# A decoder kernel on one Trainium2 core: eleven feed-forward slices and two down steps of layer 0 as seven block products

## The chip, the core and the metric

The kernel runs on one core of a Trainium2 chip. The core has a matrix engine (TensorE, PE in the profile; PEld is its weight load), VectorE (DVE), ScalarE (ACT), GpSimd (POOL) and SyncE (SP). PE reads operands from the on-chip memory SBUF and writes results to PSUM, which has eight banks of 128 x 512 float32. Sixteen DMA engines move data between DRAM and SBUF or within DRAM; SP issues nearly all loads and stores, POOL issues the indirect page loads and the sums described below. Each engine works through its own list of instructions in order and waits on semaphores for the others. The metric is device time in microseconds (us), the median of several executions.

## What is computed

A two-layer decoder step on 1024 prompt tokens and 8 sample tokens of width 1024. Layer 0 has a gated recurrence (HGRN2) and attention to 256 memory tokens, layer 1 has stick-breaking attention and memory attention; each layer ends with a SwiGLU feed-forward block of 22 slices of 128 (D_FF = 2816). Cut to the part that changes:

```python
def swiglu(h, w_gu, w_down):
    gate, up = jnp.split(h @ w_gu, 2, axis=-1)
    return (jax.nn.silu(gate) * up) @ w_down

# in run_trunk, for each layer l
h = h + rmsnorm(mix, g[1])
h = h + rmsnorm(swiglu(rmsnorm(h, g[2]), w_gu[l], w_down[l]), g[3])
```

All of it is float32. The kernel reaches that accuracy by splitting each operand into a rounded part (fp32r) and a remainder and by adding three products (high x high, high x low, low x high).

## The kernel before

The 1024 tokens are worked on in two halves, `g = 0` (512 tokens) and `g = 1` (512 tokens and the 8 samples, 520 columns in two pieces of 260). Layer 0 of the second half is woven with layer 1 of the first half, and so on: `weave` takes generators with numbers and advances the one that is furthest behind, so the program text of several stages is mixed. A scheduler then orders each engine's instructions; the text's order is its priority.

A feed-forward block runs over five parts, `PARTS = [(0, 5), (5, 5), (10, 4), (14, 4), (18, 4)]`, given as first slice and number of slices. For each slice the plain class `ffn` calls `proj` for gate and up (`L220` holds all its matmuls): it loads weights with `split_w`, four 128 x 128 tiles (256 KB) at a time into one of five `wraw` buffers, casts them on ACT (`L206`) and subtracts on DVE (`L207`), and multiplies them with the eight x tiles. `silu` is made of Exp and Ln, so that ScalarE keeps one table of functions. After the slices of a part, its down step multiplies them with `w_down` and adds into R.

The last block of the program (layer 1, second half) uses the class `ffn_w` instead. There gate and up of a slice are seen as a 2 x 2 block matrix (two halves of the 1024 inputs; gate and up) times a 2 x 2 block matrix of x (two halves of the inputs, two halves of the columns). Seven products in place of eight give the four results: each product multiplies a block or a sum of blocks of the weights by a block or a sum of blocks of x. `gate_up_w` does that with 260 columns and four 128 x 128 tiles per product (`L527`); `down_w` (`L706`) does the same for a down step with pairs of slices. The sums of x blocks (`sums_w`) are made on DVE once, those of slices (`put_sum`) as they come. Silu comes from ScalarE's own table there, which is loaded before (`L492`) and changed back behind (`L757`).

The weight sums are made in DRAM ahead of time. `weight_sums` (gate and up) and `down_sums` yield eight steps for each part, in `summed`: a copy of one block into a DRAM tile, or an accumulating DMA on top of it. Each step is paced by a one-column token: ACT copies a column of a recent result into an `rr` tile of three buffers (`L612`), POOL copies that into `mk` (`L613`), and POOL then issues the DMA (`L616` accumulates, `L618` copies). A step waits for the DMA whose result it reads. Before, only layer 1 has sums: down sums of parts 1 to 3 run beside `a1.core` (24 steps), gate and up sums beside `b0.sb`, `b0.mem` (16) and beside parts 2 to 4 of the layer 0 block of the second half (24, from about 1206 to 1410 us).

In `ffn_w` the raw weights go into the five `wraw` buffers and, from part 1 on, every other one into a half of a free `apool` tile; the split weights go into five `wspl` and some of four `cpool` tiles.

Of the kernel before, what the change touches and what calls it, by code (L numbers as in the profile page):

```python
# [18 lines left out]
P = 128  # L19
# [5 lines left out]
def tile_decoder(  # L25
# [169 lines left out]

    def split_w(W, k0, nk, m0):
        out = []
        for a in range(0, nk, 4):
            n = min(4, nk - a)
            raw = wraw.tile([P, 4, P], F32, tag="w", name=nm("w"))  # L200
            nc.sync.dma_start(
                raw[:, :n, :],
                W[(k0 + a) * P : (k0 + a + n) * P, m0 : m0 + P].rearrange("(k p) m -> p k m", p=P),
            )
            ws = wspl.tile([P, 2, 4, P], F32R, tag="ws", name=nm("ws"))
            nc.scalar.copy(ws[:, 0, :n, :], raw[:, :n, :])  # L206
            nc.vector.tensor_sub(ws[:, 1, :n, :], raw[:, :n, :], ws[:, 0, :n, :].bitcast(F32))  # L207
            for i in range(n):
                out.append((ws[:, 0, i, :], ws[:, 1, i, :]))
        return out  # L210
# [84 lines left out]
    def sums_w(xs, ops):  # L295
# [29 lines left out]
    def YT():  # L325
        return xpool.tile([P, 2, NG[1]], F32R, tag="x0", name=nm("y"))
# [172 lines left out]
    def gate_up_w(l, f, ops, spl, raws, pair=None):  # L499

        h, n = PW[1], NG[1]
        part, o = part_of(f)
        gate, up = f * P, DFF + f * P
        src = [
            (w_gu[l][0:512, gate : gate + P], 0), (sums[l][part][0][:, o : o + P], 4), (sums[l][part][1][:, o : o + P], 5),
            (w_gu[l][512:D, gate : gate + P], 1), (sums[l][part][2][:, o : o + P], 6), (sums[l][part][3][:, o : o + P], 2),
            (w_gu[l][512:D, up : up + P], 3),
        ]

        def weight(j):  # L510
            r = raws()
            nc.sync.dma_start(r, src[j][0].rearrange("(k p) m -> p k m", p=P))
            return r.rearrange("p k m -> p (k m)")

        def split(src):
            w = spl()
            nc.scalar.copy(w[:, 0, :], src)  # L517
            nc.vector.tensor_sub(w[:, 1, :], src, w[:, 0, :].bitcast(F32))  # L518
            return w

        def product(ps, j, first=False):
            w = split(weight(j))
            i = src[j][1]
            for k in range(4):
                x = ops[k][i]
                for wi, (wj, xi) in enumerate(((0, 0), (0, 1), (1, 0))):
                    nc.tensor.matmul(  # L527
                        ps[:, :h], w[:, wj, k * P : (k + 1) * P], x[:, xi, :],
                        start=(first and k == 0 and wi == 0), stop=(k == 3 and wi == 2), skip_group_check=True,
                    )  # L530
# [41 lines left out]
        return mt  # L572

# [25 lines left out]
    def down_sums(l, parts, after):  # L599
        for i in parts:  # L600
            t = [tc.dram_tile([P, 2, 512], F32, name=nm("dsum")) for _ in range(4)]
            dsums[i] = t
# [18 lines left out]
    dsums = {}  # L621
    htok, done = [], []

    PARTS = [(0, 5), (5, 5), (10, 4), (14, 4), (18, 4)]

    class ffn_w:


        def __init__(self, l, x, plain):
# [3 lines left out]
            self.sums = sums_w(x, self.ops)  # L633
# [23 lines left out]
        def gate_up(self, pi, j0=0, j1=None):  # L657
# [3 lines left out]
            for j in range(j0, nf if j1 is None else j1):  # L661
# [7 lines left out]
                else:  # L669
                    pair = pairs[j // 2] if self.block(pi) and j < 4 else None  # L670
                    mids.append(gate_up_w(l, f0 + j, self.ops, self.spl, self.raws, pair))
                yield

        def down_w(self, pi, f0, pairs, extra):
            l, n, h, R = self.l, NG[1], PW[1], self.R
            a11, a12, a21, a22 = down_blocks(l, f0)
            s1, s2, s3, s4 = dsums[pi]
            src = ((a11, 0), (s1, 4), (s2, 5), (a12, 1), (s3, 6), (s4, 2), (a22, 3))
            for m0 in (0, 2):
                ms = (m0, m0 + 1)  # L680
                acc = [[Q(i) for i in range(4)] for _ in ms]

                def weight(rows):
                    r = self.raws().rearrange("p k m -> p (k m)")
                    nc.sync.dma_start(r.rearrange("p (t c) -> p t c", t=2), rows[:, :, m0 * P : (m0 + 2) * P])
                    w = self.spl()
                    split_to((w[:, 0, :], w[:, 1, :]), r)
                    return w

                def slice_of(q, hf, a, first=False):  # L690
                    for i in range(2):
                        o = hf * 256 + i * P
                        for wi, (wj, xi) in enumerate(((0, 0), (0, 1), (1, 0))):
                            nc.tensor.matmul(
                                acc[i][q][:, :h], we[:, wj, o : o + P], extra[0][:, xi, a * h : (a + 1) * h],
                                start=(first and wi == 0), stop=(wi == 2), skip_group_check=True,
                            )

                def product(q, j, first=False):
                    w = weight(src[j][0])  # L700
                    for i in range(2):
                        for t in range(2):
                            x = pairs[t][src[j][1]]
                            o = t * 256 + i * P
                            for wi, (wj, xi) in enumerate(((0, 0), (0, 1), (1, 0))):
                                nc.tensor.matmul(  # L706
                                    acc[i][q][:, :h], w[:, wj, o : o + P], x[:, xi, :],
                                    start=(first and t == 0 and wi == 0), stop=(t == 1 and wi == 2),
                                    skip_group_check=True,
                                )  # L710

                def add(q, mo, a, sub=False):
                    for i, m in enumerate(ms):
                        d = R[m + mo][:, a * h : (a + 1) * h]
                        (nc.vector.tensor_sub if sub else nc.vector.tensor_add)(d, d, acc[i][q][:, :h])

                def minus(q, p):
                    for i in range(2):
                        nc.scalar.activation(acc[i][q][:, :h], acc[i][p][:, :h], AF.Copy, scale=-1.0)

                product(0, 0, True)
                minus(1, 0)
                product(3, 1, True)
                product(1, 2)
                minus(2, 1)
                product(0, 3)
                if extra:
                    tail = w_down[l][(f0 + 4) * P : (f0 + 5) * P, :].rearrange("p (o m) -> p o m", o=2)
                    we = weight(tail)
                    slice_of(0, 0, 0)  # L730
                add(3, 4, 1)
                add(0, 0, 0)
                product(1, 4)
                add(3, 0, 1, True)
                add(1, 4, 1)
                product(2, 5)
                if extra:
                    slice_of(2, 0, 1)
                add(2, 0, 1)
                product(1, 6)  # L740
                if extra:
                    slice_of(1, 1, 0)
                    slice_of(0, 1, 1, True)
                    add(0, 4, 1)
                add(1, 4, 0)
                yield

        def down(self, pi):
# [11 lines left out]
            if self.block(pi):  # L760
                yield from self.down_w(pi, f0, pairs, mids[4:])
                return
# [124 lines left out]
    class ffn:  # L887
        def __init__(self, g, l, xt, rows=False):
            self.g, self.l, self.xt, self.rows = g, l, xt, rows
            self.R = self.acc = None  # L890

        def part(self, pi):
            g, l = self.g, self.l
# [3 lines left out]
            mids = []  # L897
            for j in range(nf):
                pg = proj(g, w_gu[l], 0, ND, (f0 + j) * P, self.xt)
# [960 lines left out]
```

## Time and profile before

| quantity | value |
|---|---|
| median of three runs | 2425.81 us (2425.56 to 2427.13) |
| the profiled execution's own time | 2427.11 us |
| its span, first to last instruction | 2425.4 us |
| granted TensorE clock | 0.998 |
| busy share of PE, DVE, ACT, POOL | 99%, 66%, 51%, 6% |
| mean of the DMA rate | 152 GB/s |

The page's busy time of PE is modelled, as its matmuls overlap; how much the engine really did in a stretch is better seen from the chain of waits, which gives for a stretch the time and the number of matmuls that followed one another with nothing in between. The stretch of interest, parts 2 to 4 of layer 0 on the second half, is there from 1195.88 on. "q0" is the queue of the DMAs that POOL issues, "q1" that of SP.

### The profile page before, as it was taken

What the parts mean: (1) busy time and instruction counts of PE and PEld (TensorE: products, weight loads), DVE (VectorE), ACT (ScalarE), POOL (GpSimd) and SP (SyncE); (2) the same over time, 40 slices, a digit from 0 to 9 for tenths busy, and PEclk for the clock granted to TensorE, in tenths of its full rate; (3) what the DMA queues carried; (4) which work ended last, traced back from release to release, by engine and by line L of the source; (5) the groups of instructions that cost most, each with busy time, mean ns of one, the idle gap of its engine ahead of it and who ended that gap; (6) DMA issues with size and microseconds to landing.
All of it is one profiled execution on the core that took longest, in us unless ns stands there. A gap on an engine that the chain in (4) does not pass through costs nothing.

```text
span 2425.4 us, 40863 instructions
## 1 busy us (share of the span) xinstructions
PE 2402.9 (99%) x15411; PEld 2134.4 (88%) x15411; DVE 1594.4 (66%) x2776; ACT 1231.5 (51%) x2455; POOL 139.2 (6%) x215
## 2 busy tenths in 40 slices
PE   8999999999999999999999999999999999999998
PEld 6888988888877888999999989887787797999998
DVE  5777556765865676555544585777687648757885
ACT  5557544444444445555433454555454445565665
POOL 3000001200000000011111100121000000000000
PEclk9999999999999999999999999999999999999999
DMA  5353255774733445455778866644453334365652
GB/s 188 101 160 105 75 157 144 180 208 143 221 109 97 138 148 183 120 137 150 179 198 210 247 182 197 191 135 123 130 182 93 95 118 126 119 189 175 184 174 75
DMA packets 499224, 369.25 MB, mean 152 GB/s; under 512 B 19757, under 2 KB 444314, under 8 KB 499026
## 3 DMA queue, kind: packets, MB, share of 16 engines
q1 hardware_dynamic: 476008, 307.87, 42.4%
q0 software_dynamic: 22912, 58.73, 10.4%
q8 instruction: 121, 1.98, 0.3%
q14 instruction: 77, 0.63, 0.1%
q10 hardware_dynamic: 106, 0.04, 0.0%
HBM read 336.74 MB, written 80.15 MB: 172 GB/s over the span
## 4 chain that ended last, share of the span: by engine, by line
PE 91%; issue 4%; DVE 2%; ACT 1%; DMA 1%; POOL 0%; SPq 0%; DVEq 0%; POOLq 0%; ACTq 0%
PE mm L220 63%; PE q L527 7%; PE q L706 2%; PE q L485 2%; PE mm L1216 2%; PE q L770 1%; PE s L1055 1%; PE s L1014 1%; PE s L1399 1%; PE mm L968 1%; PE mm L991 1%; PE q L854 1%; PE s L1574 1%; PE s L1613 1%; PE s L1041 1%
## 5 line engine op out<-in xcount | busy, mean ns | idle before, releaser
L220 PE MATMUL mm<-x,ws 128*128 128x260 f32 (+1 forms) x7776 | 1329.0, 330 | 0.0
L220 PEld LDWEIGHTS mm<-x,ws 128*128 128x128 f32 x7776 | 1148.7, 188 | 142.6 <-issue 7.5
L206 ACT CAST ws<-w 128x512 fp32r<-128x512 f32 (+1 forms) x672 | 397.7, 592 | 638.7 <-PE mm L220 553.3
L207 DVE TENSOR_TENSOR ws<-w,ws 128x512 fp32r<-128x512 f32 (+1 forms) x672 | 438.4, 655 | 239.3 <-ACT ws L206 232.7
L220 PE MATMUL mm<-m,ws 128*128 128x512 f32 (+1 forms) x2112 | 391.2, 342 | 0.0
L220 PEld LDWEIGHTS mm<-m,ws 128*128 128x128 f32 x2112 | 323.6, 188 | 45.9 <-issue 2.3
L518 DVE TENSOR_TENSOR ws<-w,ws 128x512 fp32r<-128x512 f32 x126 | 86.6, 691 | 46.7 <-ACT ws L517 44.7
L527 PE MATMUL q<-y,ws 128*128 128x260 f32 x864 | 113.0, 283 | 0.0
L527 PEld LDWEIGHTS q<-y,ws 128*128 128x128 f32 x864 | 107.6, 188 | 0.0
L419 DVE TENSOR_TENSOR r<-r,mm 128x512 f32<-128x512 f32 (+1 forms) x96 | 66.1, 688 | 59.3 <-PE mm L220 58.1
L517 ACT CAST ws<-w 128x512 fp32r<-128x512 f32 x126 | 77.8, 618 | 47.9 <-PE q L527 15.3
L260 DVE TENSOR_SCALAR t<-mm 128x512 f32<-128x512 f32 (+1 forms) x74 | 51.2, 692 | 63.8 <-PE mm L220 63.8
L902 DVE TENSOR_TENSOR t<-t,mm 128x512 f32<-128x512 f32 (+1 forms) x66 | 45.5, 689 | 68.0 <-PE mm L220 68.0
L264 DVE TENSOR_TENSOR t<-t,t 128x512 f32<-128x512 f32 (+1 forms) x66 | 45.8, 693 | 66.9 <-ACT t L263 66.9
L527 PE MATMUL q<-x,ws 128*128 128x260 f32 x648 | 86.8, 283 | 0.0
L527 PEld LDWEIGHTS q<-x,ws 128*128 128x128 f32 x648 | 81.7, 189 | 0.0
L613 POOL COPY mk<-rr 128x1 f32<-128x1 f32 x64 | 29.6, 463 | 738.6 <-ACT rr L612 738.5
L283 DVE TENSOR_TENSOR st<-st,n 128x512 f32<-128x512 f32 (+1 forms) x91 | 62.2, 691 | 3.0 <-ACT n L282 1.5
L227 ACT CAST m<-t 128x512 fp32r<-128x512 f32 (+1 forms) x76 | 47.4, 623 | 31.2 <-DVE t L902 24.7
L261 ACT ACTIVATE t<-t 128x512 f32<-128x512 f32 (+1 forms) x66 | 42.1, 637 | 36.2 <-DVE t L260 32.0
L1152 POOL DMA_INDIRECT c<-in_cache_sb_k,pidx x16 | 20.7, 1292 | 604.5 <-DMA vsc<-c 423.7
L228 DVE TENSOR_TENSOR m<-t,m 128x512 fp32r<-128x512 f32 (+1 forms) x76 | 52.6, 692 | 2.3 <-ACT m L227 1.1
(378 smaller groups left out, 2874.1 us busy)
## 6 DMA issues: line engine op xcount, KB each, us to landing
w<-in_w_gu SPq DMA_DIRECT2D x334, 256.0 KB, 3.1
w<-in_w_down SPq DMA_DIRECT2D x156, 256.0 KB, 2.9
w<-in_w_in_a SPq DMA_DIRECT2D x80, 256.0 KB, 2.9
wsum<-in_w_gu POOLq DMA_DIRECT2D x18, 1024.0 KB, 9.6
w<-wsum SPq DMA_DIRECT2D x72, 256.0 KB, 3.6
w<-in_w_o SPq DMA_DIRECT2D x64, 256.0 KB, 2.8
dsum<-in_w_down POOLq DMA_DIRECT2D x18, 512.0 KB, 6.0
w<-in_w_mem_kv SPq DMA_DIRECT2D x32, 256.0 KB, 2.9
```

The lines of the kernel that those rows point to most:

```text
L206: nc.scalar.copy(ws[:, 0, :n, :], raw[:, :n, :])
L207: nc.vector.tensor_sub(ws[:, 1, :n, :], raw[:, :n, :], ws[:, 0, :n, :].bitcast(F32))
L220: nc.tensor.matmul(ps[:, a, : PW[g]], wt, xt[k][:, xi, o : o + PW[g]], start=(k == 0 and wi == 0), stop=(k == nk - 1 and wi == 2),)
L228: nc.vector.tensor_sub(dst[1], src, dst[0].bitcast(F32))
L260: nc.vector.tensor_scalar(sv(x, g), pv(ps, g), -44.0, None, op0=ALU.max)
L283: nc.vector.tensor_add(acc[:, :n], acc[:, :n], t[:, :n])
L419: nc.vector.tensor_add(dst, dst, pv(ps, g))
L485: nc.tensor.matmul(pp[a][:, :h], wt, xt[k][:, xi, a * h : (a + 1) * h], start=(k == 0 and wi == 0), stop=(k == ND - 1 and wi == 2),)
L517: nc.scalar.copy(w[:, 0, :], src)
L518: nc.vector.tensor_sub(w[:, 1, :], src, w[:, 0, :].bitcast(F32))
L527: nc.tensor.matmul(ps[:, :h], w[:, wj, k * P : (k + 1) * P], x[:, xi, :], start=(first and k == 0 and wi == 0), stop=(k == 3 and wi == 2), ...
L706: nc.tensor.matmul(acc[i][q][:, :h], w[:, wj, o : o + P], x[:, xi, :], start=(first and t == 0 and wi == 0), stop=(t == 1 and wi == 2), sk ...
```

## The change

Layer 0's feed-forward block of the second half (`f1 = ffn(1, 0, ...)`) becomes mixed. Slices 0 to 10 stay plain; slices 11 to 21 (`FIRST = 11`) go through `gate_up_w`, and the down steps of parts 2 and 3 through `down_w`, both now functions outside `ffn_w`, which takes the same code. PSUM is used there through the tags of the other stages: `quads` takes one `mm` tile (two banks) and two `s` tiles, `four` the same for each of two rows, with the `ns` bank. Parts are run with a lag as in layer 1: one slice of the next part stands ahead of a part's down step. `sums_w` for layer 0 writes into `apool` tiles, three of its four steps during the down step of part 1, the last behind slice 10. Raw weights use the five `wraw` buffers alone, as `free` is not given. Silu comes from its own table from slice 11 on, and the table is changed back behind the last slice.

Layer 0 needs weight sums of its own: 24 steps for gate and up (parts 2 to 4, of part 2 three slices) and 16 for the down steps of parts 2 and 3. Layer 1's sums stay the same and move. In all 104 steps stand where 64 stood:

| stage | before | after |
|---|---|---|
| `a0.mem` and `a1.fq` | 0 | 6 |
| `o0.mm` (layer 0) | 0 | 5 |
| `a1.core` and `f0.part(0)` | 24 down (layer 1) | 16 down (layer 0) |
| `a1.mem_sample` and `f0.part(2)`, `f0.part(3)` | 0 | 9 |
| `f0.part(4)` (layer 0) | 0 | 4 |
| `b0.sb`, `b0.mem` | 16 | 16 |
| parts 2 to 4 of `f1` in layer 0 | 24 | 10 |
| `b1.sb` and the samples of layer 1 | 0 | 8, and 12 down |
| `o1.mm` (layer 1) | 0 | 6, and 6 down |
| `o1.finish` | 0 | 6 down |

The token is now a column of the weight tile that was split last (`now`).

```diff
     def split_w(W, k0, nk, m0):
...
+            now[0] = ws[:, 0, 0, 0:1].bitcast(F32)
...
-        pa, pb, pc, pd = (Q(i) for i in range(4))
+        pa, pb, pc, pd = quads()
...
+    FIRST = 11
     PARTS = [(0, 5), (5, 5), (10, 4), (14, 4), (18, 4)]
...
     class ffn:
-        def __init__(self, g, l, xt, rows=False):
-            self.g, self.l, self.xt, self.rows = g, l, xt, rows
+        def __init__(self, g, l, xt, plain=NF, blocks=(), free=None):
+            self.g, self.l, self.xt, self.plain, self.blocks, self.free = g, l, xt, plain, blocks, free
...
+            self.sums = sums_w(xt, self.ops, lambda: A(F32R))
+
+        def spl(self):
+            self.n += 1
+            if self.n % 8 in (1, 4, 6):
+                return cpool.tile([P, 2, 512], F32R, tag="c", name=nm("ws"))
+            return wspl.tile([P, 2, 512], F32R, tag="ws", name=nm("ws"))
+
+        def quads(self):
+            two = mmp.tile([P, 2, 512], F32, tag="mm", name=nm("mm"))
+            return S(), two[:, 0, :], two[:, 1, :], S()
+
+        def raws(self):
+            self.r += 1
+            if self.r % 2 or not self.free:
+                return wraw.tile([P, 4, P], F32, tag="w", name=nm("w"))
...
+        def four(self, i):
+            two = mmp.tile([P, 2, 512], F32, tag="mm", name=nm("mm"))
+            return [S(), two[:, 0, :], two[:, 1, :], NS() if i else S()]
...
+        def gate_up(self, pi, j0=0, j1=None):
...
+                pair = pairs[j // 2] if pi in self.blocks else None
+                if f0 + j >= self.plain:
+                    mids.append(gate_up_w(l, f0 + j, self.ops, self.spl, self.raws, self.quads, pair))
+                    yield
+                    continue
...
+                if f0 + j == self.plain - 1 < NF - 1:
+                    drain(self.sums)
+                yield
+
+        def down(self, pi):
...
+            if last and self.plain < NF:
+                with tc.issue_after(done[-1].ins):
+                    nc.scalar.preload_act_table_set("natural_log_exp_and_others")
...
+            if pi in self.blocks:
+                yield from down_w(l, pi, self.R, pairs, mids[4:], self.raws, self.spl, self.four)
+                return
...
+                    if f0 + nf < self.plain <= f0 + nf + 1 and m > 1:
+                        next(self.sums)
...
-    weave((a0.mem(), 8), (a1.fq(), 8))
+    here = lambda: now[0]
+    ws = weight_sums(0, (2, 3, 4), here, FIRST)
+    weave((a0.mem(), 8), (a1.fq(), 8), (islice(ws, 6), 6))
...
-    weave((chain(f1.part(2), f1.part(3), f1.part(4)), 24), (ws, 24))
+    lagged = chain(
+        f1.gate_up(2), f1.gate_up(3, 0, 1), f1.down(2), f1.gate_up(3, 1), f1.gate_up(4, 0, 1), f1.down(3),
+        f1.gate_up(4, 1), f1.down(4),
+    )
+    weave((lagged, 20), (islice(ws, 10), 10))
...
-    drain(o1.mm(b1.xo))
-    weave((o1.finish(), 17), (f0.part(4), 8))
+    weave((o1.mm(b1.xo), 8), (chain(ws, islice(ds, 6)), 12))
+    weave((o1.finish(), 17), (f0.part(4), 8), (ds, 6))
```

How the rows stand now, at three places. The first is PE in the layer 0 block of the second half. Before, at the seam of a gate and an up projection (`mm` the PSUM tile, `x` the input tile, `ws` a split weight; the numbers are buffers):

```order
L220 MATMUL mm_11905<-x_9251,ws_11902 128x260 x6
L220 MATMUL mm_11905<-x_9255,ws_11902 128x260 x6
L220 MATMUL mm_11977<-x_9118,ws_11969 128x260 x6
L220 MATMUL mm_11977<-x_9122,ws_11969 128x260 x6
L220 MATMUL mm_11977<-x_9162,ws_11969 128x260 x6
```

The same engine after the change, in the first block slice: products 1 to 4 of slice 11 (`a` tiles hold sums of x blocks, `s` and `mm` are PSUM).

```order
L555 MATMUL s_12148<-a_11664,ws_12169 128x260 x6
L555 MATMUL s_12148<-a_11926,ws_12169 128x260 x6
L555 MATMUL mm_12146<-a_11662,ws_12186 128x260 x3
L555 MATMUL mm_12146<-a_11797,ws_12186 128x260 x3
L555 MATMUL mm_12146<-a_11924,ws_12186 128x260 x3
L555 MATMUL mm_12146<-a_12116,ws_12186 128x260 x3
L555 MATMUL s_12147<-x_9295,ws_12204 128x260 x3
L555 MATMUL s_12147<-x_9299,ws_12204 128x260 x3
```

A weight tile `ws` served 24 matmuls, four rows of six; now it serves 12, and the next one is due.

The second is ACT in the same stage. Before, weight casts and the three steps of a silu:

```order
L206 CAST ws_13651<-w_13649 128x512
L261 ACTIVATE t_13505<-t_13504 128x520
L262 ACTIVATE t_13505<-t_13505 128x520
L263 ACTIVATE t_13505<-t_13505 128x520
L206 CAST ws_13656<-w_13654 128x512
L206 CAST ws_13719<-w_13717 128x512
L227 CAST m_13571<-t_13505 128x520
L612 COPY rr_13578<-t_13505 128x1
```

After, in the third block slice: the copies between PSUM banks (`L562`, `L565`, `L571`) stand between casts (`L544`) of products seven or eight further on, and two tokens (`L620`) follow a cast.

```order
L562 ACTIVATE mm_12440<-s_12441 128x260
L544 CAST ws_12612<-w_12610 128x512
L544 CAST ws_12647<-w_12645 128x512
L230 CAST m_12429<-n_12368 128x260
L571 COPY t_12532<-s_12442 128x260
L544 CAST ws_12629<-w_12627 128x512
L230 CAST m_12429<-n_12368 128x260
L565 ACTIVATE mm_12440<-mm_12440 128x260
L544 CAST ws_12705<-w_12703 128x512
L620 COPY rr_12729<-ws_12705 128x1
L620 COPY rr_13016<-ws_12705 128x1
```

An evacuation of PSUM now waits in ACT's list behind casts of weights that PE needs much later.

The third is POOL where layer 1's attention of the second half begins. Before, the last steps of the layer 0 stage are followed by the page loads (`c`):

```order
L613 COPY mk_14200<-rr_14198 128x1
L618 DMA wsum_13577<-wsum_13575 512x512
L613 COPY mk_14273<-rr_14271 128x1
L616 DMA wsum_13577<-in_w_gu 512x512
L1152 DMA c_16354<-in_cache_sb_k,pidx 128x512 x2
L1152 DMA c_16462<-in_cache_sb_k,pidx 128x512 x2
```

After, twenty steps of sums stand behind the last page loads of that stage; these are the first:

```order
L1216 DMA c_17695<-in_cache_sb_v,pidx 128x512 x2
L1216 DMA c_17788<-in_cache_sb_v,pidx 128x512 x2
L621 COPY mk_17731<-rr_17729 128x1
L624 DMA wsum_14379<-in_w_gu 512x512
L621 COPY mk_17819<-rr_17817 128x1
L624 DMA wsum_14377<-in_w_gu 512x512
L621 COPY mk_17904<-rr_17902 128x1
L626 DMA wsum_14378<-wsum_14379 512x512
```

Sums that POOL had issued ahead of the layer 1 attention now start only when its page loads are through.

More of the change, by code (lines that the diff above doesn't have):

```diff
@@ L632, in __init__ @@
             self.half, self.mids = [], {}
-            self.sums = sums_w(x, self.ops)
+            self.sums = sums_w(x, self.ops, Y0)
         def spl(self):
@@ L670, in gate_up @@
                     pair = pairs[j // 2] if self.block(pi) and j < 4 else None
[L671 to L745, printed above, removed]
@@ L746, in down_w @@
+                    mids.append(gate_up_w(
+                        l, f0 + j, self.ops, self.spl, self.raws, lambda: [Q(i) for i in range(4)], pair
+                    ))
                 yield
@@ L760, in down @@
             if self.block(pi):
-                yield from self.down_w(pi, f0, pairs, mids[4:])
+                yield from down_w(
+                    l, pi, self.R, pairs, mids[4:], self.raws, self.spl, lambda i: [Q(q) for q in range(4)]
+                )
                 return
@@ new lines, in spl @@
+        def spl(self):
[10 more added lines that the diff above has]
+                return wraw.tile([P, 4, P], F32, tag="w", name=nm("w"))
+            if not self.half:
+                t = self.free()
+                self.half = [t[:, 0], t[:, 1]]
+            return self.half.pop(0)
```

165 lines of the change are left out of this document (124 added, 41 removed).

## The prediction

> **What bounds the kernel now.** I read the first page from the top, then the chain of waits, then busy time by stage, then the weight loads of two stages. The profiled execution took 2427.1 us for a span of 2425.4, so 1.7 us lie around the span; the median of the runs is 2425.8, or 1.3 below the execution that I sum from.
>
> ```profile
> span 2425.4 us, 40863 instructions
> PE 2402.9 (99%) x15411; PEld 2134.4 (88%) x15411; DVE 1594.4 (66%) x2776; ACT 1231.5 (51%) x2455; POOL 139.2 (6%) x215
> PE 91%; issue 4%; DVE 2%; ACT 1%; DMA 1%; POOL 0%; SPq 0%; DVEq 0%; POOLq 0%; ACTq 0%
> ```
>
> TensorE carries 91% of the chain that ended last. The next fence is the chain in order of time, with the stretch that the change rewrites (layer 0, second half of the tokens, slices 10 to 21) and two stretches of layer 1, where block products already run.
>
> ```profile
> 1195.88 209.81 PE mm L220 x1730
> 2150.20 50.48 PE q L527 x420
> 2277.19 20.11 PE q L706 x168
> ```
>
> In all three nothing but TensorE is on the chain: 209.81/1730 = 0.121, 50.48/420 = 0.120 and 20.11/168 = 0.120 us for one matmul of 260 columns. So a matmul of 260 columns is worth 0.120 us wherever TensorE is kept fed, and layer 1 shows that gate_up_w (L527) and the block down projection (L706) can be fed. Whether layer 0 can feed them is the question, and two things differ there. These are the stages by window, the first the layer 0 stretch, the second the start of layer 1's second half, the third its block products:
>
> ```profile
> core 0: us, PE busy (x) PEld busy (x) DVE busy (x) ACT busy (x) POOL busy (x), PEclk, DMA share, GB/s
> 1194.00:1406.00 212.00, 212.00 (x1744) 210.46 (x1742) 104.63 (x153) 85.11 (x156) 32.10 (x49) 1.00 0.83 213
> 2054.00:2150.00 96.00, 95.42 (x782) 93.97 (x783) 63.78 (x132) 50.75 (x112) 0.00 (x0) 0.98 0.45 133
> 2150.00:2380.00 230.00, 230.00 (x1916) 230.00 (x1915) 181.11 (x362) 144.05 (x306) 0.00 (x0) 1.00 0.59 175
> ```
>
> Layer 1 has no weight sums running (POOL x0); its block products alone take 0.59 of the 16 DMA engines. The layer 0 stretch has them running (POOL x49) at a DMA share of 0.83. After the change both loads meet in one stage.
>
> **The change, part by part.** *Fewer matmuls.* A plain slice is 2 x 8 x 3 x 2 = 96 matmuls, a block slice 7 x 4 x 3 = 84; eleven slices save 132. A plain down step with four rows of slices is 8 x 4 x 3 x 2 = 192, a block step 2 x 7 x 12 = 168; two steps save 48. 180 x 0.120 = -21.6 us, all on the path.
>
> *More weights a microsecond.* A block product consumes a 256 KB weight tile in 12 x 0.120 = 1.44 us, where the plain path takes 2.88. Layer 1 reads through the five wraw buffers and through halves of free apool tiles in turn; the new class gets no free tiles, so only the five. A ring of five turns in 7.2 us. In it must fit the issue, the landing, the cast and the subtraction. These are the landing times of the weight loads in layer 1's block stage, then in the layer 0 stretch, and the two group lines of the split:
>
> ```profile
> DMA to landing us min/median/max: 2.7/3.3/4.3
> DMA to landing us min/median/max: 3.7/5.9/11.5
> L518 DVE TENSOR_TENSOR ws<-w,ws 128x512 fp32r<-128x512 f32 x126 | 86.6, 691 | 46.7 <-ACT ws L517 44.7
> L517 ACT CAST ws<-w 128x512 fp32r<-128x512 f32 x126 | 77.8, 618 | 47.9 <-PE q L527 15.3
> ```
>
> Without sums: 3.3 + 0.62 + 0.69 = 4.6 us plus some 0.4 for the issue, so 2.2 us are spare. With sums: 5.9 + 1.7 = 7.6, and 0.4 are missing. Why the landing doubles is seen in the DMA rows of the layer 0 stretch. The first two rows are POOL's timeline: an accumulating sum is issued at 1254.79, and the next step waits for it until 1264.10. The third is the sums' queue q0 in the 10 us from 1254 on, the next two all that moved in the 3 us from 1258, the last one 1.5 us (from 1238.5) behind another sum. The columns of a queue's row are packets, MB and the share of 16 engines.
>
> ```profile
> 1254.79 1.02 POOL L616 DMA_DIRECT2D wsum<-in_w_gu  x1 [2.59 <-DMA wsum<-wsum]
> ...
> 1264.10 0.66 POOL L618 DMA_DIRECT2D wsum<-wsum  x1 [6.15 <-DMA wsum<-in_w_gu]
> ...
> q0 software_dynamic: 529, 1.05, 58.4%
> ...
> DMA packets 302, 0.62 MB, mean 206 GB/s; under 512 B 0, under 2 KB 0, under 8 KB 302
> q0 software_dynamic: 302, 0.62, 112.0%
> ...
> q1 hardware_dynamic: 935, 0.47, 108.1%
> ```
>
> One accumulate holds the 16 engines for 0.584 x 10 = 5.8 us, and for 3 us of it no packet of the weight queue q1 moves at all; behind it q1 catches up with 0.47 MB in 1.5 us. A plain copy between DRAM tiles holds them for less; the row is the 11 us from 1287 on, with one copy (29.7% of 11 = 3.3):
>
> ```profile
> q0 software_dynamic: 272, 1.05, 29.7%
> ```
>
> In the new stage stand ten of these steps where 24 stood: four accumulates and six copies, one about every 19 us. A cast that waits for a late weight holds what stands behind it on ScalarE: the copies between PSUM banks (L562, L565, L571), for which the third and sixth product wait. Casts run seven or eight products ahead, but those evacuations stand behind them, so that lead does not protect TensorE; only the spare 2.2 us do. Bounds: nothing, if the spare time swallows each; 4 x (5.8 - 2.2) + 6 x (3.3 - 2.2) = 21 at the most. The median landing with sums is nearest (0.4 us missing per turn of the ring, one or two turns for an accumulate, part of it swallowed by the 1.44 us of a product that needs no copy): I take 1.25 us for each accumulate, none for a copy: +5.
>
> The Trainium skill ("DMA: Bandwidth & Descriptors", section "Queues, rings and completion order") says that each DMA engine goes round its queues in turn, a packet of each at a time. By that a waiting weight load would keep moving beside a sum, and this term would be nearer 0 than 5, the sum some 4 us lower. The 3 us with 302 packets of q0 and none of q1 do not agree, though in the windows beside them both queues move.
>
> *Operand sums in layer 0.* 16 quarters of sums_w: 48 DVE operations and 16 casts of 260 columns more, during the end of the attention stage. Layer 1 does the same work in the window 2054 to 2150, where TensorE is busy for 95.42 of 96.00. So 0 to 5 us; I take 1.
>
> *ScalarE tables.* Silu in layer 0 adds two table loads (before: L492 and L757, one each). The row of the first one, which lies in that same full window:
>
> ```profile
> L492 ACT ACT_TABLE_LOAD  x1: 1283/1283/1283, 2061.2 to 2061.2; - x1
> ```
>
> 0 to 2.6 us; I take 0.5, as TensorE did not pause there. The Trainium skill ("ScalarE: Activation LUTs", section "What ACT_TABLE_LOAD costs") counts about 2.66 us a switch with the drain; by it the upper end would be 5.3. The load itself agrees to the nanosecond.
>
> *Sums in other stages.* 64 steps become 104. In the stages with the first half (512 columns a matmul; first row below, 11.09/48 = 0.231 us) a weight lasts 12 x 0.231 = 2.8 us and the ring 13.9, so about 9 us are spare, more than an accumulate holds. The a1.core stage had 24 such steps and the second row shows TensorE full; it now has 16. New ones: 6 and 5 around the first output projection, 9 beside a1.mem_sample, 4 in f0.part(4), 20 in layer 1's attention stage, behind the page gathers on POOL in program order. The risk there is not weights but the sample loads, prefetched by one:
>
> ```profile
> 394.14 11.09 PE mm L220 x48
> ...
> 365.00:545.00 180.00, 179.73 (x1031) 152.67 (x1030) 121.27 (x226) 83.24 (x178) 27.75 (x48) 1.00 0.71 178
> ...
> DVE c L1118 <- DMA c<-in_cache_mem_v: 12.8, 9, 2.5
> ```
>
> VectorE waited 2.5 us at most for one. Some eight loads met by a sum could add up to 1.3 us each: -1 to +10, I take 2.
>
> *The dense place.* The output projection of layer 1's second half (1940 to 1988, 48 us) gets twelve steps, one per 4 us, six of 1 MB and six of 0.5 MB, most of them chained:
>
> ```profile
> wsum<-in_w_gu POOLq DMA_DIRECT2D x18, 1024.0 KB, 9.6
> ...
> dsum<-in_w_down POOLq DMA_DIRECT2D x18, 512.0 KB, 6.0
> ...
> 1940.00:1988.00 48.00, 48.00 (x383) 46.75 (x382) 16.65 (x25) 19.74 (x35) 0.00 (x0) 1.00 0.41 128
> ```
>
> From 1254.79 to 1264.10 one chained step took 9.3 us, so POOL falls behind, and the token copies (L620) on ScalarE, with three buffers, wait for it; weight casts stand behind these. Four or five steps fit before that happens. 0 to 8; I take 2.
>
> Sum: -21.6 + 5 + 1 + 0.5 + 2 + 2 = -11.1. From 2427.1 that is 2416.0; from the median 2414.7, the predicted time.
>
> **The rivals.** *All cover holds* (0.22): the spare 2.2 us and the PSUM double buffering swallow the sums, as the layer 0 stretch now shows no pause at all despite 24 steps. -21.6 plus 1 or so: 2405. Against it: there the ring has 14.4 us.
>
> *The weight ring starves TensorE* (0.20, slower): one mechanism, the five wraw buffers under running sums. In full the ten steps hold the engines for 4 x 5.8 + 6 x 3.3 = 43 us. If two thirds of that reach TensorE (29 us), the time is 2425.8 - 21.6 + 29 + 5.5 = 2438.7. It decides from about 21 us, half of the hold. For it: q1 needs 0.59 of the engines all the time, and sums leave it none. Against it: they are 19 us apart and the queue catches up at full rate.
>
> *The gain is eaten* (0.16, no change): starvation of 10 to 20 us, or late sample loads of 10 us in layer 1's attention stage: 2421 to 2431. For it: the landing maximum of 11.5 with sums; against it: its median.
>
> **How the numbers follow.** A measurement of this kernel can tell about 0.2% (4.9 us) from no change. My forecast, gain less partial stalls (2409 to 2421), has 0.42; all covered 0.22; together faster 0.64, same 0.16, slower 0.20. The range 2403 to 2431 holds all but the starved case.
>
> **What would show it.** Right: 180 matmuls fewer; in the layer 0 stretch about 1550 matmuls in some 192 us, with short pauses of TensorE, each beginning a few microseconds behind an accumulate on POOL, and ScalarE's split casts (L544) waiting for DMA there; a1.core as full as now. Wrong: no pauses there (2405), or casts waiting for weights also between the sums (ring too short by itself), or VectorE's waits for c loads grown by tens of microseconds, or token copies on ScalarE waiting for POOL in the output projection.

## The result, and the profile after

The changed kernel takes 2467.8 us (median of four, 2464.5 to 2471.4) where the kernel before takes 2425.7 beside it: ratio 1.0175, 95% interval 1.0163 to 1.0187. It is slower by 42 us, where 11 us less were forecast. The first page of the changed kernel:

```profile
span 2467.3 us, 41133 instructions
PE 2402.6 (97%) x15231; PEld 2125.9 (86%) x15231; DVE 1644.8 (67%) x2944; ACT 1277.2 (52%) x2612; POOL 187.6 (8%) x295
PE 83%; DMA 7%; DVE 6%; ACT 2%; issue 2%; POOL 0%; DVEq 0%; SPq 0%; ACTq 0%
```

There are 15411 - 15231 = 180 matmuls fewer, as counted, and TensorE's share of the chain falls from 91% to 83%: DMA, VectorE and ScalarE have taken over. Where, is read from marks that both programs have: the first scaling of R in each residual (L400 before, L403 after). This is how much later than before each stretch ends, less what it started with:

| stretch (us in the trace before) | after minus before |
|---|---|
| start to `o0.finish` (331) | -1.1 |
| to `f0.finish` (841): a1.core, samples of layer 0 | +10.7 |
| to `f1.finish` (1409): b0, then the block products of layer 0 | +25.5 |
| to `o1.finish` of layer 1 (1990): its attention and samples | +7.1 |
| to the end | -0.4 |

The block stage, from the multiplication of the last plain slice (slice 10) to the last evacuation of the last down step, took 195.4 us before. Less 21.6 for 180 matmuls it should take 173.8; it takes 213.3. Another 7.7 us are lost just ahead of it, between slices 9 and 10 (63.9 us for 56.2). The views of waits from 1204 to 1441, first the five largest of TensorE, then the three largest of ScalarE for DMAs (total us, times, longest):

```profile
PE mm L555 <- ACT mm L565: 11.6, 3, 4.5
PE mm L555 <- DVE t L573: 8.4, 4, 5.4
PE s L1119 <- ACT b L1110: 4.6, 1, 4.6
PE mm L662 <- DVE r L671: 2.5, 4, 0.9
PE mm L555 <- DVE t L575: 2.0, 2, 1.7
```

```profile
ACT ws L544 <- DMA w<-wsum: 25.1, 9, 5.7
ACT ws L230 <- DMA w<-dsum: 14.3, 4, 5.7
ACT ws L544 <- DMA w<-in_w_gu: 13.8, 6, 6.0
```

No row, nor one of the same view for TensorE's weight loads, says that TensorE waits for a split weight (`ws`). Each of these five ends with a copy or addition that empties PSUM, while ScalarE waits 53 us for raw weights in its three. One such pause in the chain of waits, and the same moment in ScalarE's timeline:

```profile
1257.26 11.57 DMA w<-dsum
...
1269.37 0.40 ACT ys L230
1269.77 0.28 ACT mm L565
1270.10 2.97 PE mm L555 x12
...
1279.95 1.43 PE mm L662 x12
```

```profile
1262.57 0.61 ACT L230 CAST ws<-w 128x512 fp32r<-128x512 f32 x1
1268.85 0.62 ACT L230 CAST ws<-w 128x512 fp32r<-128x512 f32 x1 [5.66 <-DMA w<-dsum]
1269.37 0.40 ACT L230 CAST ys<-n 128x260 fp32r<-128x260 f32 x1
1269.68 0.37 ACT L565 ACTIVATE mm<-mm 128x260 f32<-128x260 f32 x1
```

A weight of the next down step lands 11.6 us after its issue. Its cast holds ScalarE for 5.66 us, and `L565` of the present slice, 0.37 us long, stands behind it. Then the next twelve matmuls take 2.97 us, where twelve take 1.43 further on.

In the layer 0 sample stage long loads end up on the chain of waits; two of them are shown first. VectorE's waits for such loads follow, from 605 to 790 (before, in the same stage: 8.7 and 1.1 us in all).

```profile
612.14 9.79 DMA n<-qd
...
746.44 8.19 DMA c<-in_cache_mem_v
```

```profile
DVE c L1182 <- DMA c<-in_cache_mem_v: 17.0, 5, 5.5
DVE c L1166 <- DMA n<-qd: 6.9, 1, 6.9
```

The dense place is untouched: with twelve steps beside it, TensorE is full in the output projection of layer 1.

```profile
1982.00:2030.00 48.00, 48.00 (x383) 46.80 (x382) 16.38 (x25) 21.10 (x45) 9.92 (x19) 1.00 0.89 234
```

### The profile page after: what moved, and what is told of

The parts are those of the page before. It is cut to its first block, busy times and chain, and to the rows that moved or that the text cites. A ratio compares the mean times of both kernels' runs of the same rounds, so it can differ in the third digit from the quotient of the medians.

```text
span 2467.3 us, 41133 instructions
## 1 busy us (share of the span) xinstructions
PE 2402.6 (97%) x15231; PEld 2125.9 (86%) x15231; DVE 1644.8 (67%) x2944; ACT 1277.2 (52%) x2612; POOL 187.6 (8%) x295
## 4 chain that ended last, share of the span: by engine, by line
PE 83%; DMA 7%; DVE 6%; ACT 2%; issue 2%; POOL 0%; DVEq 0%; SPq 0%; ACTq 0%
PE mm L223 53%; PE q L555 7%; PE q L662 2%; PE q L488 2%; PE mm L1280 2%; PE mm L555 2%; DMA w<-wsum 1%; DMA n<-qd 1%; PE q L783 1%; DMA w<-in_w_gu 1%; PE s L1119 1%; PE s L1463 1%; PE mm L1032 1%; DMA w<-dsum 1%; PE s L1078 1%
## 5 line engine op out<-in xcount | busy, mean ns | idle before, releaser
L223 PE MATMUL mm<-x,ws 128*128 128x260 f32 (+1 forms) x6720 | 1206.6, 338 | 2.7 <-DVE t L948 2.7
L223 PEld LDWEIGHTS mm<-x,ws 128*128 128x128 f32 x6720 | 1025.3, 189 | 146.9 <-issue 10.6
L208 ACT CAST ws<-w 128x512 fp32r<-128x512 f32 x612 | 360.1, 590 | 495.2 <-PE mm L223 415.4
L209 DVE TENSOR_TENSOR ws<-w,ws 128x512 fp32r<-128x512 f32 x612 | 396.7, 651 | 214.5 <-ACT ws L208 209.9
L223 PE MATMUL mm<-m,ws 128*128 128x512 f32 (+1 forms) x1728 | 346.4, 356 | 1.6 <-DVE r L422 1.3
L223 PEld LDWEIGHTS mm<-m,ws 128*128 128x128 f32 x1728 | 278.2, 189 | 48.3 <-issue 2.8
L545 DVE TENSOR_TENSOR ws<-w,ws 128x512 fp32r<-128x512 f32 x203 | 139.3, 691 | 84.1 <-ACT ws L544 80.8
L544 ACT CAST ws<-w 128x512 fp32r<-128x512 f32 x203 | 124.3, 618 | 108.1 <-DMA w<-wsum 29.3
L621 POOL COPY mk<-rr 128x1 f32<-128x1 f32 x104 | 44.0, 423 | 1483.0 <-ACT rr L620 1483.0
L422 DVE TENSOR_TENSOR r<-r,mm 128x512 f32<-128x512 f32 (+1 forms) x80 | 54.9, 686 | 35.9 <-PE mm L223 34.9
L555 PE MATMUL mm<-a,ws 128*128 128x260 f32 x396 | 59.0, 302 | 13.5 <-ACT mm L565 11.6
L230 ACT CAST ws<-w 128x512 fp32r<-128x512 f32 x72 | 44.2, 617 | 46.0 <-DMA w<-dsum 14.3
L555 PEld LDWEIGHTS mm<-a,ws 128*128 128x128 f32 x396 | 53.7, 204 | 16.1 <-ACT mm L565 12.2
```

Source lines behind the costliest of these rows:

```text
L223: nc.tensor.matmul(ps[:, a, : PW[g]], wt, xt[k][:, xi, o : o + PW[g]], start=(k == 0 and wi == 0), stop=(k == nk - 1 and wi == 2),)
L230: nc.scalar.copy(dst[0], src)
L422: nc.vector.tensor_add(dst, dst, pv(ps, g))
L555: nc.tensor.matmul(ps[:, :h], w[:, wj, k * P : (k + 1) * P], x[:, xi, :], start=(first and k == 0 and wi == 0), stop=(k == 3 and wi == 2), ...
L621: mark = nc.gpsimd.tensor_copy(small([P, 1], tag="mk", bufs=1), tok)
```

## The experiments

Each ran beside the kernel before, whose median was 2424.7 to 2425.8. "Block stage" is the time defined above; "early" and "late" are the differences of the table's stretches. The theory at the start (A): weight sums on queue q0 starve the raw ring of five. The rival (B): that ring is too short without any sums.

**e1: no sums in the block stage.**

```diff
-    weave((lagged, 20), (islice(ws, 10), 10))
+    drain(lagged)
...
+    weave((kv_proj(1, xk1), 8), (islice(ws, 4), 4))
...
+    weave((b1.heads(), 8), (o0.finish(), 17), (islice(ws, 6), 6))
```

> Edit: the ten sum steps that stand beside the layer 0 block products (parts 2 to 4 of f1) are taken out of that stage; four go beside kv_proj and six beside b1.heads, right behind it, where matmuls are plain and a raw weight lasts 2.88 us. Nothing else changes. Theory A (sums starve the ring: the weight queue q1 has to share the DMA engines with q0 while the five wraw buffers last only 7.2 us): TensorE's pauses and half-speed matmuls in the layer 0 stretch, about 49 us of excess over 0.120 us a matmul, fall under 10; the stretch takes 190 to 198 us instead of 236; time 2422 to 2432. Theory B (the ring of five is too short by itself, since pauses at 1306 and 1367 us have no sum near): at least half of the excess stays, time 2445 or more.

2438.7 us (ratio 1.0066, 1.0047 to 1.0085), between the two cases. The stretch of the block stage ends 8.7 us early instead of 25.5 late, but the stage takes 185.5 us, 11.7 more than its matmuls. So sums are most of it, and without them something remains, in which ScalarE still waits for loads though no sum runs beside them:

```profile
ACT ws L544 <- DMA w<-wsum: 14.4, 8, 3.1
ACT ws L544 <- DMA w<-in_w_gu: 7.8, 6, 3.4
```

The stretch to which the ten steps went is 10.0 late where it was 7.1; that may be their price, but the same stretch differs by more between runs that leave its sums alone (1.3 in e11).

**e2: no sums beside the layer 0 samples.**

```diff
-    weave((a1.core(), 22), (f0.part(0), 9), (down_sums(0, (2, 3), here), 16))
+    weave((a1.core(), 22), (f0.part(0), 9), (chain(down_sums(0, (2, 3), here), islice(ws, 9)), 25))
...
-        (islice(ws, 9), 9),
```

> Edit: the nine sum steps beside a1.mem_sample go to the end of the a1.core stage, which then has 25 (it had 24 before the change). Theory A (the sums delay the sample loads, prefetched by one): VectorE's waits for c loads and n loads of that stage fall back from 31 and 17 us to about 13 and 3, the stage is 9 to 10 us shorter, time 2457 to 2460. Rival (the stage is longer for another reason, or the delay moves into a1.core): time 2465 or more.

2463.0 us (1.0151, 1.0134 to 1.0168), between the two cases. VectorE's waits for `c` loads fall from 17.0 to 9.5 us, as theory A has it, yet the stretch is still 10.7 late: the rival's second half. The delay moved into a1.core. POOL's timeline there, then what TensorE waited for:

```profile
471.04 0.66 POOL L626 DMA_DIRECT2D wsum<-wsum  x1 [8.79 <-ACT ws L208]
...
477.73 1.01 POOL L624 DMA_DIRECT2D wsum<-in_w_gu  x1 [5.84 <-DMA wsum<-wsum]
```

```profile
PE s L1500 <- ACT b L1496: 7.9, 1, 7.9
```

POOL waits for the sum that the next one reads, ScalarE's token copies wait for POOL's three `rr` buffers, and one evacuation stands behind them. That is what the prediction feared for the output projection, at another place.

**e3: a raw ring of ten.** Every other raw weight takes half a `cpool` tile; the split weights lose those tiles.

```diff
+    f1 = ffn(1, 0, o1.x, FIRST, (2, 3), lambda: cpool.tile([P, 2, 4, P], F32, tag="c", name=nm("w")))
...
-            if self.n % 8 in (1, 4, 6):
+            if self.n % 8 in (1, 4, 6) and not self.free:
```

> Edit: in the layer 0 block every other raw weight goes into a half of a cpool tile, and the split weights use wspl alone: raw ring ten products deep (14.4 us a turn instead of 7.2), split ring five deep (instead of seven to eight). The sums stay where they are. Theory A with the ring as its size: a turn then equals that of the plain slices, which showed no pauses beside 24 sums; the excess in the stretch falls from 49 to 5 to 15 us, time 2424 to 2434. If it is the total lead in front of TensorE that counts (raw plus split, 12.5 products before, 15 now), the excess falls by some 20 percent only, time 2455 to 2462. If casts that stand far ahead of their use hold the PSUM copies on ScalarE, the shorter split ring alone helps by more than half.

2432.9 us (1.0032, 1.0023 to 1.0042), the block stage 190.4 us with all ten sums in it. The edit changes two things, a longer raw ring and a shorter split ring; e10 takes them apart.

**e4: sums in small packets.**

```diff
+                for r in (slice(0, 256), slice(256, 512)) if pk else (slice(None),):
+                    if add:
+                        nc.gpsimd.dma_start(d[r], a[r], accum_op=ALU.add, **pk)
...
```

(`pk` holds `max_dma_last_dim=512` for layer 1's sums of gate and up.)

> Edit: the gate and up sums of layer 1 (the ten in the layer 0 stretch and the others) are cut into pieces of 512 bytes, each step issued as two DMAs; bytes moved, places and order stay. Theory A1 (the queues take turns packet by packet, so the weights' 512 byte and 1 KB packets get a third of the bytes or less beside packets of 2 and 4 KB): weights then get half or more, the pauses in the stretch fall by a third to a half, time 2445 to 2456. Theory A2 (the engines' time is what is shared, whatever the packets; smaller packets make a sum only longer): the sums last longer, the pauses stay or grow, time 2467 to 2485.

2472.1 us (1.0185, 1.0168 to 1.0202): by the time, theory A2. By stretch it is both. The block stage is faster, 206.0 us for 213.3, and its stretch 10 us better. The queues' rows while a sum runs beside down weights, first of the changed kernel (12 us from 1259), then of e4 (2 us from 1255, where two loads had been issued at 1253.17 and 1255.70):

```profile
q0 software_dynamic: 906, 1.82, 84.0%
q1 hardware_dynamic: 846, 0.82, 25.5%
```

```profile
q0 software_dynamic: 512, 0.26, 114.5%
q1 hardware_dynamic: 4, 0.00, 0.9%
```

In the changed kernel the queues move nearly as many packets each, and the bytes follow from their sizes: beside 2 KB packets the weights get 0.82 MB in 12 us, 68 KB/us, where block products consume 256 KB in 1.44 us. In e4 the sum's packets go ahead alone, and the weights catch up behind them (554 packets against 157 in the 2.5 us from 1258.5). So the shares change within one sum, and e4 is no clean test of theory A1; why the sum goes first stays open. But the stretch with layer 1's attention gets 20 us worse, as POOL falls behind: the chain at the output projection.

```profile
2007.90 1.84 POOL wsum L625
2009.74 8.28 issue
...
2020.75 0.03 ACT rr L620
2020.77 0.06 issue
...
2020.86 0.58 ACT a L420
2021.44 0.04 issue
2021.48 16.96 PE mm L223 x108
```

There the dense place fails as the prediction described it: POOL late, token, ScalarE, TensorE.

**e5: e1 and e3 together.**

> Edit: the edits of e1 (the ten sums out of the layer 0 block stage) and of e3 (raw ring ten deep, split ring five deep) together; it closes the square of the two causes. Measured by the time at which the layer 0 block's finish begins, against the kernel before and less the shift that the stage starts with: the change 25.5 us late, e1 8.7 early, e3 5.1 early; the matmuls saved are worth 21.6. If ring and sums are one cause (a ring that is deep enough needs no quiet engines, and the other way round), e5 is no earlier than e1 by more than 4 us, 9 to 13 early. If the ring of five costs some 12 us of its own, e5 is 17 to 21 early. Whole time: 2425 to 2430 in the second case, 2433 to 2437 in the first; the waits of the sample stages (10 us in layer 0, 7 to 10 in layer 1) stay in both.

2430.6 us (1.0019, 1.0009 to 1.0028); the stretch is 13.9 us early, between the two cases, the stage 181.7 us.

**e6 and e7: sums spread**, the moved ones two to four a stage, over the stages without samples or block products (`o1.mm` and `o1.finish` of the second half take five more); ten instead of twenty stay in layer 1's attention stage. e7 has the rings of e3 as well.

```diff
-    weave((lagged, 20), (islice(ws, 10), 10))
+    drain(lagged)
...
-        (chain(iter(range(16)), islice(ws, 8), islice(ds, 12)), 40),
+        (chain(iter(range(16)), islice(ws, 3), islice(ds, 7)), 28),
```

> Edit: no sums in the layer 0 block stage, none beside a1.mem_sample, ten instead of twenty in layer 1's attention stage; they go, two to four a stage, to o0.finish, f0.finish, kv_proj, b0.heads, b0.sb, and the same stages of the second half; ring of five as in the change. If the sums beside the sample loads are the cause, the layer 0 sample stage is 0 to 2 us longer than before the change instead of 10.8, and layer 1's attention stage 2 to 4 longer instead of 7.1; the block stage stays as in e1 (8.7 us early). Whole time 2417 to 2425. If the lateness there has another cause (16 down sums in a1.core, POOL's backlog), the sample stage stays over 6 us long: time 2427 or more.

> Edit: e6 with the deep raw ring of e3. The block stage should gain 17 to 21 us if the ring of five has a cost of its own, 9 to 13 if not, the sample stages as in e6. Whole time 2407 to 2416 in the first case (faster than the kernel before by 10 to 18 us), 2417 to 2423 in the second.

e6: 2424.0 us (0.9993, 0.9983 to 1.0003). e7: 2417.4 us (0.9966, 0.9953 to 0.9978). The stretch with the layer 0 samples is 5.4 and 2.7 us late instead of 10.7, more than the 0 to 2 of e6's first case, though e6's time lies in its range. The block stage takes 187.3 and 181.2: the rings of e3 are worth 6 us without sums too, and e7's time falls into the second case, in which the ring of five has no such cost of its own.

**e8: three steps out of `o0.finish`; e9: negated copies on VectorE.**

```diff
-    weave((o0.finish(), 17), (chain(a1.v(), a1.qm(A)), 8), (islice(ws, 3), 3))
+    weave((o0.finish(), 17), (chain(a1.v(), a1.qm(A)), 8))
```

```diff
-        nc.scalar.activation(pb[:, :h], pa[:, :h], AF.Copy, scale=-1.0)
+        neg(pb[:, :h], pa[:, :h])
```

(`neg` is `nc.vector.tensor_scalar` with a factor of -1 in layer 0 and the old line in layer 1.)

> Edit: e7 with the three steps of o0.finish moved ahead of it (two to a0.mem and a1.fq, one to o0.mm). TensorE paused 5.7 us there in e7 and 3.7 in the kernel before; if these steps are the rest of the lateness at the first landmark behind the layer 0 sample stage (2.6 us), it falls to about 0.5 and the time to 2414 to 2416. If not, it stays at 2417.

> Edit: e8, and in the layer 0 block slices the two negated copies between PSUM banks go from ScalarE to VectorE. If the 3 to 4 us that the third and sixth products still wait in e7 come from these copies standing behind casts and splits in ScalarE's list, the block stage is 2 to 4 us shorter (178 to 179 us from the last plain slice to the last down evacuation, instead of 181), time 1 to 4 us below e8. If VectorE's own list holds them as long (its subtractions wait for the same weights), no difference or up to 4 us more.

e8: 2412.4 us (0.9949, 0.9936 to 0.9963), the sample stretch 0.2 us early. e9: 2409.8 us (0.9934, 0.9920 to 0.9947), the stage 178.8 us after 181.2. Both go the way of their first case, e8 further than its 2414 to 2416. e9 is faster than both kernels, by 16 us and by 58. Its page:

```profile
span 2407.8 us, 41142 instructions
PE 92%; DVE 3%; DMA 2%; ACT 1%; issue 1%; POOL 0%; DVEq 0%; SPq 0%; ACTq 0%
```

**e10: the split ring alone.** The changed kernel, with the effect of e3's last line: the condition under which a split weight takes a `cpool` tile is `False`.

> Edit: the changed kernel, with the split weights of the layer 0 block in wspl alone (five instead of seven to eight); the raw ring stays at five, the sums stay. List theory (in the changed kernel TensorE's pauses end with PSUM evacuations that stand behind casts of weights needed much later, so that the lead of the split weights protects nothing): the block stage, 213 us from the last plain slice to the last down evacuation, stays within 6 us of that, time 2462 to 2474. Lead theory (what counts is how many products of weights lie in front of TensorE, raw and split together): each long pause behind a sum grows by up to 2.5 products, 3.6 us, six of them, the stage takes 225 to 235 us, time 2480 to 2490.

2441.8 us (1.0065, 1.0049 to 1.0082): neither theory. Taking the `cpool` tiles away from the split weights, with raw ring and sums as they were, makes the kernel 26 us faster; the stage takes 198.4 us, and between slices 9 and 10 it is 56.1. ScalarE's waits there (1204 to 1441):

```profile
ACT ws L544 <- PE mm L555: 17.0, 15, 2.0
...
ACT ws L230 <- DMA w<-dsum: 9.2, 4, 3.5
...
ACT ws L544 <- DMA w<-wsum: 6.3, 2, 4.5
```

Casts now wait mostly for TensorE to free a split buffer, not for loads. What TensorE waits for is less than half of what it was, most of it behind the down step's copy `L675`:

```profile
PE mm L662 <- ACT mm L675: 7.9, 3, 4.2
PE mm L555 <- ACT mm L565: 3.0, 1, 3.0
PE mm L555 <- ACT mm L562: 1.4, 5, 0.3
```

The instruction lists of the two kernels say why. For each copy between PSUM banks, take the cast ahead of it on ScalarE whose weight TensorE uses last, and count in TensorE's order how many products that weight lies behind the product whose result is copied:

| copy, eleven slices | changed kernel (and e1) | e10 (and e3) |
|---|---|---|
| `L562` | 8 to 13 | 4 to 6 |
| `L565` | 6 to 11 | 5 or 6 |

With more split buffers the scheduler puts casts further ahead, and each of them makes the copy behind it depend on a later load. Buffers behind the cast lengthen that dependence. Raw buffers ahead of it absorb some of a late load: from e10 to e3, where only the raw ring grows, the stage falls from 198.4 to 190.4 us. Of the 22.9 us that e3 gains in the stage, 14.9 are the shorter split ring's and 8.0 the longer raw ring's. A run that changes ScalarE's order and keeps the buffers was not made; that the order is the link rests on these lists and waits.

**e11: e9's edit alone, on the changed kernel.**

> Edit: the changed kernel, and only the two negated copies of the layer 0 block slices on VectorE instead of ScalarE. TensorE's idle time of 11.6 us that ends with a copy of ScalarE has to end otherwise. If ScalarE's list is the whole of the matter, it goes, and the time is 2453 to 2459. If VectorE's subtractions wait for the same casts, the copies wait there, and it stays: 2464 to 2472.

2462.4 us (1.0161, 1.0144 to 1.0178), between the two cases; the stage takes 213.9 us, no gain in it. The lines are six further on here, `L564` is the copy:

```profile
PE mm L555 <- DVE mm L564: 15.7, 4, 5.9
PE mm L555 <- DVE t L579: 7.7, 4, 6.6
```

VectorE's subtractions wait for the same casts (28.6 us in all behind `L544`); the copy waits in that list instead. The 5 us that the whole kernel gains lie mostly in layer 1's attention (1.3 late instead of 7.1), which this edit does not touch.

**e12: e9 without the deep raw ring.**

> Edit: e9 without the deep raw ring: five raw and five split buffers, sums out of the block stage, negated copies on VectorE. If the lead of the casts in ScalarE's list was what cost the time and five raw buffers are enough where no sums run, the block stage takes the 178.8 us of e9 within 1.5 us, time 2408 to 2412. If the raw ring of five has a cost of its own, as the 11.7 us lost in e1 seemed to say, the stage takes 183 us or more, time 2414 to 2420.

2412.2 us (0.9945, 0.9931 to 0.9959), the stage 178.9 us, the same as e9. ScalarE's only waits of the stage for weights (1204 to 1415), and the stage by window:

```profile
ACT ws L208 <- DMA w<-in_w_o: 1.4, 1, 1.4
ACT ws L544 <- DMA w<-in_w_gu: 0.3, 1, 0.3
```

```profile
1206.00:1385.00 179.00, 178.85 (x1453) 175.72 (x1453) 141.90 (x286) 101.13 (x201) 1.06 (x2) 1.00 0.61 179
```

With five split buffers and these copies on VectorE, five raw buffers are enough where no sums run, and B falls. Of the 11.7 us that e1 still lost, 6.6 are gone here. The rings took 4 to 6 of such a loss (e1 to e5, e6 to e7) and the moved copies 2.4 (e8 to e9); 5.1 are left.

## Why the prediction was wrong, point by point

- *Fewer matmuls, -21.6.* Right in count; each is worth 0.120 us. The best stage, 178.8 us (e9), is still 5 us above 173.8. No long wait makes that up: 54 intervals from one matmul to the next are of 0.15 to 0.3 us, where 0.12 is usual. What they wait for stays open.
- *The ring of five, +5 (bounds 0 and 21).* This step failed. It measured 39.5 us in the stage and some 6.5 ahead of it (7.7 less the operand sums). Of the whole stretch, e1 shows 34 us gone with the sums, e10 23 us gone with the sums left in. The price was taken from the ring's turn and its spare 2.2 us per turn, and the bound from the time for which a sum holds the engines. That evacuations stand behind casts was seen, and that the lead does not protect TensorE. But the lead was read as seven or eight products; it is up to 13, and it was not seen that it does harm by itself: 14.9 us of the stage go with two or three split buffers fewer, 8.0 more with five raw buffers more. Nor did the working hold a second price: after each of the four pauses over 3 us, 14 to 26 matmuls take about 0.22 us in place of 0.12, 79 in all, 8 us.
- *Which products wait.* The prediction named the third and the sixth. The three pauses behind `L565` stand at the fifth, which writes the bank that `L565` still has to read. 10.4 us more end with VectorE's `L573` and `L575`, which it did not name.
- *The Trainium skill's rule on turns by packet* ("DMA: Bandwidth & Descriptors", "Queues, rings and completion order"). The prediction held 3 us without a packet of q1 against it. In them one load had been issued, at 1257.93, and its first packet moved at 1261.49; so the objection stands for the start of a sum, as in e4's two us with 512 packets and 4. Further into a sum, 906 and 846 packets agree with the rule. The conclusion drawn from it, that the term would be nearer 0, is wrong all the same, since equal packets of unequal size left the weights a third of the bytes.
- *Operand sums, +1.* 0.9 us by the last evacuation of part 1's down step, 1.3 us in e1 by slice 10: right. *Tables, +0.5*: no wait of TensorE ends with one; nothing larger is seen.
- *Sums in other stages, +2 (bounds -1 and 10).* Failed in size: +10.7 in layer 0, of which nothing is left without the nine steps and with none in `o0.finish` (e8, e9, e12: -0.2 to 0.5). The place, sample loads prefetched by one, was right; the price of 1.3 us for each load that meets a sum was not, single waits reach 6.9 us. Layer 1's attention adds 7.1 in the changed kernel, but with the same twenty steps 1.3 to 6.5 in e2, e3, e10 and e11, and 0.6 to 2.2 with ten (e6 to e9, e12): their share is not settled.
- *The dense place, +2.* 0 in the changed kernel. The mechanism is real (e2, e4), at a higher load of POOL.
- *The rival that came true* is the starved ring, on the side and at the stage it named. Its 2438.7 was too low: it took two thirds of 43 us, 29, where the stage alone lost 39.5, and it left 2 us for the sums in other stages, where layer 0's samples alone took 10.7. Its mechanism, the five raw buffers, is the smaller part (8.0 us from e10 to e3), and e12 shows no cost of it without sums.

## What to carry to other kernels

When an in-order engine both prepares operands ahead of time and empties accumulators, buffers behind the preparation can let the scheduler move it further ahead, and tie today's evacuation to a later load (26 us of this kernel, e10). Put the slack ahead of that engine, not behind it. Price a background DMA stream by its packets against those of the stream beside it, and keep it away from stages whose loads are prefetched by one (10.7 us here). When a bottleneck engine's pauses never end with its own operands, look at what stands ahead of the releasing instruction in the other engine's list.

## What was not expected of the hardware

A long pause of TensorE costs more than itself. Those of 3.1, 3.9, 4.5 and 5.4 us in the block stage are followed by 14 to 26 slow matmuls of 260 columns, the first of 0.38 us and the others of about 0.22; behind the two of 1.6 and 1.7 us there the clock stays full. The granted clock shows it: it is the third number from the end, 0.70 in the 10 us around one of the long pauses.

```profile
1265.00:1275.00 10.00, 5.45 (x27) 5.25 (x26) 2.40 (x5) 2.73 (x7) 0.00 (x0) 0.70 1.03 250
```

The Trainium skill ("TensorE: Matmul & The Clock Gate", section "HAM oscillation — how this bites in real kernels") asks for no idle gap over some 3.4 us, behind which the array runs at half rate. The traces agree in kind, but the length is no sharp bound in them. The same pause of 1.8 us (TensorE's `L488` waits for VectorE's `L422`) is followed by a slower clock in e7 and not in e8, the first and the second row; one of 3.1 us in e11 leaves it full, the third.

```profile
2044.00:2050.00 6.00, 5.57 (x28) 4.72 (x29) 4.64 (x8) 2.30 (x4) 0.00 (x0) 0.72 0.25 74
...
2041.00:2047.00 6.00, 5.78 (x43) 5.34 (x44) 6.00 (x11) 4.04 (x7) 0.00 (x0) 1.00 0.29 81
...
750.00:765.00 15.00, 11.85 (x69) 8.78 (x68) 7.70 (x14) 4.45 (x14) 0.00 (x0) 1.00 0.44 130
```
